# Hybrid attention encoder: scores from 64-row products of two heads in turn, q and k split into high parts and rests without copies

## The chip, the cores and the metric

One core of a Trainium2 chip runs the whole layer in one launch. The metric is the device time of that launch in microseconds (us). TensorE (PE) multiplies, and its weight loads are shown as PEld; VectorE is DVE, ScalarE ACT, GpSimd POOL; SyncE (SP) issues the DMAs.

## What is computed

One encoder layer on two inputs, a sample of 2048 tokens and a prompt of 512, model width 1024, in float32. Cut to what matters here:

```python
h = rms_norm(x, norm_gain)
proj = jnp.einsum('bld,de->ble', h, w_in)        # 9216 columns
# branch a: 2-D neighbourhood attention, 8 heads of 64, window 8 rows x 16 columns, with a bias
q_a, k_a = rms_norm(q), rms_norm(k)
s = einsum(q_a, k_a) / 8 + bias; p = softmax(s); o_a = p @ v
# branch b: three groups (window, dilation) = (128,1), (512,4), (2048,16), 8 heads of 64 each
q, k = rope(rms_norm(q)), rope(rms_norm(k))
s = einsum(q, k) / 8; p = softmax(s) in the band; o = p @ v   # the groups are merged by their lse
br_a = (o_a * silu(g_a)) @ w_branch_a; br_b = (o_b * silu(g_b)) @ w_branch_b
y = x + (sigmoid(m_a) * br_a + sigmoid(m_b) * br_b) @ w_out
```

The norm gains of q and k are large, so scores are computed from split numbers: each of q and k is kept as a high part in fp16 and a rest in fp16, and a score is the sum of three products: high by rest, high by high, rest by high.

## The kernel before

The program is written by a planner: functions are queued by due time in `Clock` (lines 108 to 171), which keeps an estimated time of each engine, and buffers are granted by `Slots` (lines 174 to 236). The calls to matmul, activation and so on are emitted in the order in which the planner runs them, and each engine executes its instructions in that order. PE's estimate for a matmul is columns/2400 + 0.003 us (`mm`, line 350); a change of tile shape is not in it. All matmuls have line 351, most DVE work 364, ACT 359, POOL 376, and the transposing DMAs, which SP issues, line 399 (`turn`).

The stages follow each other on PE. `dil_sweeps` (line 1249): 60 tiles of 128 tokens, each projected to q, k and v (3 banks of 512 columns, 24 matmuls each); `dil_qk` (1358) squares, normalises and ropes q and k, splits them into `qs`, and turns them by DMA into `dq` (queries) and the ring `kT` (keys). `dil_block` (1501) then attends: 30 blocks have 256 keys per query, 36 have 128 (12 of these with only 64 queries). Eight heads make a block, in units of two heads by 256 keys or four heads by 128, so that a unit fills one PSUM bank of 512 columns (`s`, two banks). `na_sweeps` (895): 40 tiles, four heads at a time; `na_qk` (980) and `na_group` (1083), with units of one head by 512 or 384 keys (sample) or two heads by 256 (prompt); the q there is turned into `qn` and reordered by DVE into `qT`. After that `gate_sweeps` (1567) and `out_sweep` (1996) compute no scores.

A unit goes through `head` (764): score matmuls into a bank; DVE adds the mask and takes the maximum (`top`, which frees the bank); ACT takes the exponential; the result is split in two fp16 parts `p`, turned by DMA to `pT`, and multiplied with v into `o` (`pump`, 824). Up to two units are at work between score and reduction, one bank each. A unit's heads have the same parity (0 and 2, say).

The layout of the operands decides the shape of a score matmul. `parts_q` (742) writes q's high part twice for each head, side by side, and the rests of all heads after that; `parts_k` (749) writes for each pair of heads high, rest, rest, high. After the turn, one head of q is 128 partitions (high, high), one head of k 128 partitions (high and rest, in an order that depends on parity). `score` (755) then needs two matmuls: one over 128 rows for high by high plus high by rest, one over the 64 rows of the head's half for rest by high.

Buffers that the change touches (lines 57 to 78): `vc` (gathered v of the neighbourhood sweeps), `dq`, `qs` and `qn`.

Of the kernel before, what the change touches and what calls it, by code (L numbers as in the profile page):

```python
# [13 lines left out]
F32 = mybir.dt.float32  # L14
F32R = mybir.dt.float32r
BF16 = mybir.dt.bfloat16
FP16 = mybir.dt.float16
# [51 lines left out]
NE = 2  # L69
NHB = 2  # L70
NQS = 2
NOSB = 2
NV2 = 1
NQN = 2
NBM = 4
WT = 13
WA = 6
WD = 12
M_T = 0.5
M_L = 1.0  # L80
M_S = 0.0
M_CS = 6.0
NA_STEP = 2.3
NA_LAST = 1.2
NA_P = 0.7
# [22 lines left out]
class Clock:  # L108
# [34 lines left out]
    def first(self, **costs):  # L143

        return min(costs, key=lambda e: max(self.now, self.free[e]) + costs[e])
# [114 lines left out]
def size(ap):  # L260
    return math.prod(ap.shape[1:])


class Enc:


    def __init__(self, ctx, tc, a):
        self.ctx, self.tc, self.nc, self.a = ctx, tc, tc.nc, a
        clk = self.clk = Clock()
# [21 lines left out]
        self.values = deque()  # L291
        self.unit_at = 0.0

    def load_const(self, ap, shape, name):
# [444 lines left out]

    def parts_q(self, x, out, nh):

        x = x.rearrange("p (h d) -> p h d", d=64)
        hi = out[:, 0:128 * nh].rearrange("p (h r d) -> p h r d", r=2, d=64)
        lo = out[:, 128 * nh:192 * nh].rearrange("p (h d) -> p h d", d=64)
        return (hi, x.unsqueeze(2).to_broadcast([128, nh, 2, 64])), (lo, x, hi[:, :, 0])

    def parts_k(self, x, out, nh):

        x = x.rearrange("p (a e d) -> p a e d", e=2, d=64)
        z = out[:, 0:128 * nh].rearrange("p (a z d) -> p a z d", z=4, d=64)
        return (z[:, :, 0::3], x), (z[:, :, 1:3], x, z[:, :, 0::3])

    def score(self, out, q, k, h, sel, m):

        nh = sel
        pp = slice(64 * (h % 2), 64 * (h % 2) + 64)
        self.mm(out, q[:, h, :m], k, True, False)
        self.mm(out, q[pp, nh + h // 2, :m], k[pp], False, True)  # L760

    def head(self, time, u):
# [5 lines left out]
        def score():  # L770
            u["s"] = self.new("s", [128, 512])
            u["scores"](u["s"])
            self.values.append(u)
            clk.then(S["e"].take, top)

        def top():
            e = u["e"] = self.new("e", [128, 512])
# [41 lines left out]
            u["ready"] = True  # L819
            self.pump()  # L820

        clk.at(time, S["s"].take, score)

    def pump(self):

# [154 lines left out]
    def na_qk(self, R, seq, i, ps):  # L980

        clk, S = self.clk, self.S
# [20 lines left out]
            clk.then(S["qs"].take, split)  # L1003

        def split():
            qs = R["qs"] = self.new("qs", [128, 1536], FP16)
            R["q"] = self.parts_q(R["x"][:, 0:256], qs[:, 0:768], 4)
            R["k"] = self.parts_k(R["x"][:, 256:512], qs[:, 768:1280], 4)
            self.gains.when(gain)
            self.act(*R["q"][0])  # L1010
            clk.then(low_q)
# [23 lines left out]
        def turn_q():  # L1035
            if i // 4 not in seq["qT"]:
                seq["qT"][i // 4] = None
                S["qT"].take(new_q)
            R["qn"] = self.new("qn", [128, 6, 128], FP16)
            self.turn(R["qn"], R["qs"][:, 0:768])  # L1040
            moved.signal()
            clk.then(seq["q_gate"][i // 4].when, order)

        def new_q():
            seq["qT"][i // 4] = self.new("qT", [128, 6, 4, 8, 16], FP16, self.N["qT"])
            seq["q_gate"][i // 4].signal()

        def order():
# [7 lines left out]
        def turn_k():  # L1056
            if "kT" not in seq:
                pool, sfx = (self.N["kTs"], "") if tok == 0 else (self.N["kTp"], "p")
                seq["kT"] = pool.tile([128, 4, 64 * seq["rows"]], FP16, name=f"kT{sfx}")
            self.turn(seq["kT"][:, :, 128 * i:128 * i + 128], R["qs"][:, 768:1280])  # L1060
            moved.signal()
            there.signal()

# [19 lines left out]
    def na_group(self, seq, g):  # L1083

        clk, S = self.clk, self.S
        half, tok, rows = seq["half"], seq["tok"], seq["rows"]
        last = rows // 8 - 1
        lo = 0 if g == 0 else 8 * g - 4
        hi = 8 * g + 8 if g == last else 8 * g + 12
        nr = hi - lo  # L1090
# [43 lines left out]
        def unit(time, c, hs):  # L1134
            st = sts[c]
            kc = (0, 8, 24, 32)[c]
            n = 32 * nr
            u = {"m": 128, "n": n, "hs": hs, "first": hs[0] == 0, "v": lambda: st["v"], "sc": self.sc[0], "st": st}
            bm = [bms[(0, 1, 1, 2)[c], h] for h in hs]

            def scores(s):
                q = qT.rearrange("p j c r e -> p j c (r e)")[:, :, c]
                for j, h in enumerate(hs):
                    self.score(s[:, n * j:n * j + n], q, kT[:, h, lo:hi, kc:kc + 32], h, 4, 128)
                    left["scores"] -= 1
                    if left["scores"] == 0:
                        S["qT"].give(qT)
                    seq["scored"].signal()

            def topped():  # L1150
# [40 lines left out]
                if c == 3 and seq["last"]:  # L1191
                    self.na_done.signal()

            u.update(scores=scores, topped=topped, den=den, mask=lambda j: bm[j]["bm"], out=out)
            if hs[-1] == 3:
                u["last"] = lambda: S["osb"].take(finish)

            def go(j=0):
                if j < len(hs):
                    bm[j]["gate"].when(go, j + 1)  # L1200
                else:
                    self.head(0.0, u)

            clk.at(time, go)
# [8 lines left out]
        for c, hs in order:  # L1213
            ct = (0, 1, 1, 2)[c]
            if hs[0] == 0:
                clk.at(t - 5.0, seq["stored"][hi // 2 - 1].when, start, c)
            if c != 2:
                for h in hs:
                    bms[ct, h] = {"uses": 2 if c == 1 else 1, "gate": Gate(clk)}
                    clk.at(t - 3.5, self.bias_ready[half].when, S["bm"].take, bias, ct, h)  # L1220
            unit(t, c, hs)
            t += (NA_LAST if seq["last"] else NA_STEP) * len(hs) * (NA_P if nr == 8 else 1.0)
        self.unit_at = t


# [132 lines left out]
    def dil_qk(self, R, i, ps):  # L1358

        clk, S, H = self.clk, self.S, R["H"]  # L1360
        B = {}
# [40 lines left out]
            clk.then(S["qs"].take, high)  # L1402

        def high():
            B["qs"] = self.new("qs", [128, 1536], FP16)
            B["parts"] = (self.parts_k if i else self.parts_q)(B["x"], B["qs"], 8)
            self.act(*B["parts"][0])
            clk.then(low)

# [4 lines left out]

        def turn():
            for out, rows in R["to", i]():
                self.turn(out, B["qs"][rows, 0:1024 if i else 1536])
            S["qs"].give(B["qs"])
            R["ch"]["done"][R["i"]].signal()

# [9 lines left out]
    def dil_plan(self, R):  # L1430
# [6 lines left out]
            R["place", j] = Gate(clk)  # L1437

        def q_tile():
            return self.new("dq", [128, 12, 128], FP16, self.D["qT"])  # L1440

        def new_k():
            ch["slot"][i] = self.blocks % 4
# [57 lines left out]
    def dil_block(self, R, srcs, m, q, ks, vs, mask, free):  # L1501
# [6 lines left out]
        def unit(h0):  # L1508
# [1 line left out]
            hs = tuple(range(h0, h0 + 2 * nh, 2))  # L1510

            def scores(s):
                for j, h in enumerate(hs):
                    self.score(s[:m, n * j:n * j + n], q(), self.ring[:, h, ks()], h, 8, m)

            def osb():
                if "osb" not in st:
# [8 lines left out]
            def store():  # L1526
# [8 lines left out]
                if self.blocks_left == 0:  # L1535
                    self.dil_done.signal()

            u = {"m": m, "n": n, "hs": hs, "first": h0 == 0, "st": st, "v": vs, "scores": scores, "sc": self.sc[1],
                 "mask": lambda j: mask, "topped": lambda: None, "out": lambda j: st["o"][:, 64 * hs[j]:64 * hs[j] + 64],
                 "mx": lambda: osb()[:m, 512 + h0:511 + h0 + 2 * nh:2], "den": lambda j: osb()[:m, 520 + hs[j]:521 + hs[j]]}  # L1540
            if hs[-1] == 7:
# [94 lines left out]
    def gate_o(self, H, br, blk):  # L1636
# [20 lines left out]
            self.mw_gate.when(self.merge, 2 * blk + tt, o, lambda: clk.then(S["qs"].take, high, tt, o))  # L1657

        def high(tt, o):
            qs = self.new("qs", [128, 1536], FP16)  # L1660
            self.act(qs[:, 0:512], o)
            clk.then(low, tt, o, qs)

# [479 lines left out]
```

## Time and profile before

| | |
|---|---|
| median of 3 runs | 2948.18 us (2947.4 to 2948.27) |
| the profiled execution | 2953.89 us, of which the span from first to last instruction is 2952.1 us |
| mean granted TensorE clock | 0.978 of full speed |
| PE busy | 2799.5 us (20153 matmuls, each with its load) |
| DVE, ACT, POOL busy | 1611.3, 1345.0, 1273.4 us |
| DMA | 429.60 MB, its one large queue at 64.5% of 16 engines' span |

Times count from the first instruction. A row of a group gives the line, the engine, the operation, out<-in by the program's names, the tile of the array for matmuls (128*128 is rows by columns), the shape of what is streamed (128x256: partitions by columns), the count, busy us, mean ns of one, and then the idle time of the engine just before, with what ended it. A matmul's end is modelled, so that what a matmul costs is read from one start to the next. "s" is the bank of scores (and, in the gate sweeps, of another product), "proj" that of projections, "o" that of the attention's output, "mx" the maximum of a reduced score.

### The profile page before, as it was taken

Reading aid. Unit: us, or ns where it says so; the run is one execution under the profiler, and the core shown is the slowest. Engines: PE = TensorE matmul, PEld = TensorE weight load, DVE = VectorE, ACT = ScalarE, POOL = GpSimd, SP = SyncE. Lnnn points to the kernel's source line nnn. Section 1 sums busy time; section 2 is a strip of 40 time slices with the busy share of each in tenths; the row PEclk is TensorE's granted clock in tenths of the full one; section 3 lists DMA queues with packets and bytes.
Section 4 is the critical chain, followed back from the end, with each engine's and each line's share of the span. In section 5 each row is a group of like instructions: output and inputs, shape, how many; then the busy total and the mean of one; then the engine's idle time right before and its main releaser. Section 6 shows DMA issues by size and latency. Waiting matters only on the chain.

```text
span 2952.1 us, 54403 instructions
## 1 busy us (share of the span) xinstructions
PE 2799.5 (95%) x20153; PEld 1821.3 (62%) x20153; DVE 1611.3 (55%) x3894; ACT 1345.0 (46%) x3492; POOL 1273.4 (43%) x1797
## 2 busy tenths in 40 slices
PE   6999999999999999988988788899999999999999
PEld 2444444444444444444545445699999999999887
DVE  6777767776554744336777578622244544444111
ACT  5667666566565655544565466421122211222110
POOL 4777776776767777733555455200001000011110
PEclk9999999999999999999999898899999999999999
DMA  7999996867665765559999999622234443453443
GB/s 230 203 207 195 195 196 116 167 130 126 112 123 109 148 110 104 104 127 187 195 198 196 172 209 200 154 51 65 72 114 119 137 131 109 126 168 107 151 150 107
DMA packets 864459, 429.60 MB, mean 146 GB/s; under 512 B 747200, under 2 KB 791872, under 8 KB 857792
## 3 DMA queue, kind: packets, MB, share of 16 engines
q1 hardware_dynamic: 864192, 426.12, 64.5%
q8 instruction: 158, 2.59, 0.4%
q14 instruction: 109, 0.89, 0.1%
HBM read 171.72 MB, written 79.13 MB: 85 GB/s over the span
## 4 chain that ended last, share of the span: by engine, by line
PE 59%; DVE 6%; DMA 6%; ACT 3%; issue 2%; POOL 1%; SPq 1%; DVEq 0%; ACTq 0%; POOLq 0%
PE proj L351 46%; PE s L351 12%; DMA pT<-p 3%; DVE p L364 2%; PE o L351 2%; DVE e L364 2%; ACT e L359 1%; DMA qn<-qs 1%; DMA hb<-htd 1%; DMA wr<-in_w_in 1%; DMA kT<-qs 1%; SPq L394 1%; DVE wt L364 1%; POOL qk L376 0%; DVE wm L364 0%
## 5 line engine op out<-in xcount | busy, mean ns | idle before, releaser
L351 PEld LDWEIGHTS <-hb 128*128 128x128 f16 x6240 | 577.0, 99 | 601.4 <-issue 50.6
L351 PE MATMUL proj<-wt,hb 128*128 128x512 f16 (+2 forms) x3360 | 702.2, 358 | 14.6 <-DMA hb<-htd 14.6
L351 PE MATMUL proj<-wu,hb 128*128 128x512 f16 x2880 | 670.0, 383 | 11.6 <-DVE wu L364 10.1
L359 ACT ACTIVATE e<-e,neg,sc 128x256 f32<-128x256 f32 (+4 forms) x688 | 394.7, 575 | 11.1 <-DVE neg L364 3.6
L359 ACT ACTIVATE sg<-proj,wi 128x256 f32<-128x256 f32 x240 | 113.2, 473 | 612.5 <-PE proj L351 606.4
L351 PE MATMUL proj<-hb,wt 128*128 128x256 f16 x2760 | 313.8, 273 | 1.6 <-DMA hb<-htd 1.6
L351 PEld LDWEIGHTS <-pT 128*128 128x128 f16 (+1 forms) x4560 | 223.3, 100 | 130.6 <-DMA pT<-p 59.0
L351 PEld LDWEIGHTS <-wt 128*128 128x128 f16 x2760 | 269.0, 98 | 34.7 <-issue 2.6
L364 DVE TENSOR_TENSOR p<-e,p 128x512 f16<-128x512 f32 (+2 forms) x304 | 256.4, 844 | 44.0 <-ACT p L359 41.0
L376 POOL TENSOR_TENSOR sq<-qk,gcs 128x256 f32<-128x256 f32 x240 | 184.0, 788 | 223.3 <-DVE q_ssq L364 212.1
L364 DVE TENSOR_TENSOR qk<-s,sg 128x256 f32<-128x256 f32 x160 | 67.8, 424 | 336.4 <-PE s L351 333.4
L364 DVE CAST p<-e 128x512 f16<-128x512 f32 (+2 forms) x234 | 141.1, 603 | 195.0 <-ACT e L359 170.0
L351 PE MATMUL s<-hb,wt 128*128 128x256 f32 x1880 | 247.1, 285 | 0.0
L351 PE MATMUL proj<-hb,kT 128*128 128x256 f16 x1920 | 228.5, 275 | 5.5 <-DVE kT L364 3.5
L351 PEld LDWEIGHTS s<-hb,wt 128*128 128x128 f32 x1880 | 231.3, 189 | 1.0
L351 PE MATMUL s<-kT,dq 64*128 64x256 f16 (+5 forms) x1056 | 209.3, 254 | 3.0 <-DMA kT<-qs 3.0
L364 DVE CUSTOM_DVE_ANT_0 e<-s,cmask 128x256 f32<-128x256 f32 (+2 forms) x528 | 157.3, 343 | 96.0 <-PE s L351 92.3
L351 PEld LDWEIGHTS <-kT 128*128 128x128 f16 x1920 | 183.9, 99 | 31.6 <-DVE kT L364 5.0
L351 PEld LDWEIGHTS <-dq 64*128 64x128 f16 (+3 forms) x1056 | 101.8, 96 | 136.9 <-issue 54.6
L376 POOL TENSOR_TENSOR hb<-sg,hb 128x256 fp32r<-128x256 f32 x19 | 18.8, 989 | 381.2 <-ACT hb L359 381.1
L376 POOL TENSOR_TENSOR qk<-qk,sq 128x512 f32<-128x512 f32 (+1 forms) x122 | 167.2, 1370 | 34.6 <-DVE qk L364 25.1
L359 ACT ACTIVATE qs<-qk 128x1024 f16<-128x1024 f32 (+1 forms) x200 | 140.3, 706 | 84.0 <-POOL qk L376 65.4
(182 smaller groups left out, 3899.0 us busy)
## 6 DMA issues: line engine op xcount, KB each, us to landing
hb<-htd SPq DMA_DIRECT2D x40, 1024.0 KB
wr<-in_w_in SPq DMA_DIRECT2D x132, 256.0 KB
obd<-osb SPq DMA_DIRECT2D x50, 264.0 KB
hd<-xs SPq DMA_DIRECT2D x20, 512.0 KB
htd<-hb SPq DMA_DIRECT2D x10, 1024.0 KB
mad<-qk SPq DMA_DIRECT2D x40, 256.0 KB
e<-obd SPq DMA_DIRECT2D x40, 256.0 KB
sq<-mad SPq DMA_DIRECT2D x40, 256.0 KB
```

Of the source, the lines that this page charges most:

```text
L351: self.nc.tensor.matmul(out, a, b, start=start, stop=stop)
L359: self.nc.scalar.activation(out, x, func, **kw)
L364: getattr(self.nc.vector, ins)(out, *a, **kw)
L376: getattr(self.nc.gpsimd, ins)(out, *a, **kw)
L394: self.nc.sync.dma_start(out=out, in_=in_)
```

## The change

q and k are each split once into high parts of all heads and rests of all heads, without the second copies (`parts` takes the place of `parts_q` and `parts_k`; 1024 columns for 8 heads in both, where q had 1536). Each score is three matmuls over 64 rows, high by rest, high by high, rest by high. `head` now takes two units, of even and odd heads, whose matmuls alternate between the lower and the upper 64 rows and between the two banks; both banks are taken before the first matmul. The neighbourhood units are paired likewise (heads 0 and 1, 2 and 3; in the prompt (0, 2) with (1, 3)). The planner counts half of a matmul's time for one of a pair, and 0.3 us for each pair. Four buffers are deeper. Functions that only follow the new shapes (`qs`, `qn`, `qT`, `dq` with 1024, 4, 4 and 8 in place of 1536, 6, 6 and 12) are left out here.

```diff
-NVC = 3
+NVC = 4
-NDQ = 4
+NDQ = 6
-NQS = 2
+NQS = 3
-NQN = 2
+NQN = 3
+SWITCH = 0.3
...
-    def mm(self, out, a, b, start, stop):
-        self.nc.tensor.matmul(out, a, b, start=start, stop=stop)
-        self.clk.pe(size(b) * (4 if b.dtype == F32 else 1) / 2400 + 0.003)
+    def mm(self, out, a, b, start, stop, share=1, **kw):
+        self.nc.tensor.matmul(out, a, b, start=start, stop=stop, **kw)
+        self.clk.pe((size(b) * (4 if b.dtype == F32 else 1) / 2400 + 0.003) / share)
...
+    def parts(self, x, out, nh):
+        hi, lo = out[:, 0:64 * nh], out[:, 64 * nh:128 * nh]
+        return (hi, x), (lo, x, hi)
+
+    def score(self, banks):
+        for j in range(max(len(b) for b in banks)):
+            for i, (x, y) in enumerate(((0, 1), (0, 0), (1, 0))):
+                for bank in banks:
+                    out, q, k, h, n, m = bank[j]
+                    pp, c = slice(64 * (h % 2), 64 * (h % 2) + 64), h // 2
+                    self.mm(out, q[pp, c + x * (n // 2), :m], k[pp, c + y * (n // 2)], i == 0 and j == 0, i == 2,
+                            share=len(banks), skip_group_check=True)
+        self.clk.pe(SWITCH)
...
+    def head(self, time, *us):
+        clk, S = self.clk, self.S
+        def score():
+            self.score([u["scores"](u["s"]) for u in us])
+            for u in us:
+                u["scored"]()
+                self.values.append(u)
+                clk.then(S["e"].take, self.softmax, u)
+        def first():
+            us[0]["s"] = self.new("s", [128, 512])
+            if len(us) == 1:
+                score()
+            else:
+                S["s"].take(second)
+        def second():
+            us[1]["s"] = self.new("s", [128, 512])
+            score()
+            self.pairs.popleft()
+            if self.pairs:
+                clk.then(S["s"].take, self.pairs[0])
...
         if nr == 8:
-            order = [(c, (e, 2 + e)) for c, e in ((0, 0), (0, 1), (1, 0), (2, 0), (1, 1), (2, 1), (3, 0), (3, 1))]
+            order = [(c, ((0, 2), (1, 3))) for c in range(4)]
         else:
-            order = [(c, (h,)) for c, h in
-                     ((0, 0), (0, 1), (0, 2), (0, 3), (1, 0), (1, 1), (2, 0), (2, 1), (1, 2), (1, 3), (2, 2), (2, 3),
-                      (3, 0), (3, 1), (3, 2), (3, 3))]
+            order = [(c, ((h,), (h + 1,))) for c, h in ((0, 0), (0, 2), (1, 0), (2, 0), (1, 2), (2, 2), (3, 0), (3, 2))]
...
-        clk.at(t, S["osb"].take, lambda: [self.head(clk.now + step * j, u) for j, u in enumerate(us)])
+        clk.at(t, S["osb"].take, lambda: [self.head(clk.now + step * j, *us[j:j + 2]) for j in range(0, len(us), 2)])
```

What followed `score` in `head` before is now `softmax`, one unit at a time and otherwise the same.

## Rows read from the trace of the kernel before

**Rows 1.** Page, span and part 1: busy time, share of the span, instructions.
```profile
span 2952.1 us, 54403 instructions
PE 2799.5 (95%) x20153; PEld 1821.3 (62%) x20153; DVE 1611.3 (55%) x3894; ACT 1345.0 (46%) x3492; POOL 1273.4 (43%) x1797
```

**Rows 2.** Busy time by stretch, all engines.
```profile
core 0: us, PE busy (x) PEld busy (x) DVE busy (x) ACT busy (x) POOL busy (x), PEclk, DMA share, GB/s
170.00:450.00 280.00, 273.21 (x1823) 128.80 (x1821) 201.69 (x469) 194.85 (x507) 201.30 (x276) 1.00 0.92 191
450.00:1260.00 810.00, 801.77 (x5047) 384.93 (x5047) 464.83 (x1260) 489.07 (x1383) 590.59 (x855) 0.99 0.65 122
1260.00:1895.00 635.00, 538.20 (x4243) 303.53 (x4242) 442.11 (x1091) 353.05 (x938) 293.68 (x458) 0.92 0.92 185
1895.00:2952.00 1057.00, 1053.37 (x8372) 944.79 (x8369) 377.97 (x798) 199.80 (x423) 81.71 (x70) 1.00 0.38 115
```

**Rows 3.** Chain that ended last, shares by line: 450 to 1260, then 1400 to 1895 us.
```profile
by line: PE proj L351 45.6%; PE s L351 9.7%; ACT e L359 3.8%; PE o L351 3.6%; issue 2.3%; DMA kT<-qs 1.8%; DVE p L364 1.8%; DVE e L364 1.7%; POOL qk L376 1.6%; SPq L399 0.9%; ACT qs L359 0.8%; DVE wt L364 0.7%; DVE q_ssq L364 0.7%; DVE qs L
...
by line: PE proj L351 18.3%; DMA pT<-p 15.4%; issue 8.5%; DVE p L364 7.1%; DVE e L364 6.3%; PE s L351 5.2%; DMA qn<-qs 4.8%; PE o L351 3.3%; DMA hb<-htd 3.0%; SPq L394 2.0%; DVE qT L364 1.9%; DVE oparts L364 1.8%; ACT e L359 1.7%; POOL q_t 
```

**Rows 4.** Timeline of PE, dilated sweep: start us, us, instructions.
```profile
485.43 3.40 PE L351 MATMUL proj<-wt,hb 128*128 128x512 f16 x15
488.67 0.91 PE L351 MATMUL s<-kT,dq 128*128 128x256 f16 x4
489.51 0.82 PE L351 MATMUL proj<-wt,hb 128*128 128x512 f16 x3
490.17 0.86 PE L351 MATMUL o<-dv,pT 128*128 128x64 f16 x24
```

**Rows 5.** Timeline of PE: a unit of 128 columns, then one of 512.
```profile
905.58 1.34 PE L351 MATMUL s<-kT,dq 128*128 128x128 f16 x8
906.85 2.76 PE L351 MATMUL proj<-wu,hb 128*128 128x512 f16 x12
...
1442.54 0.69 PE L351 MATMUL s<-kT,qT 128*128 128x512 f16 x2
1443.16 0.52 PE L351 MATMUL o<-vc,pT 128*128 128x64 f16 x12
```

**Rows 6.** Groups by form, PEld: busy us, mean ns.
```profile
L351 PEld LDWEIGHTS <-pT 128*128 128x128 f16 x4272 | 212.4, 99 | 120.1 <-DMA pT<-p 57.6 <-issue 11.2
```

**Rows 7.** Score matmuls (tile s) on PE by stretch: span, busy (count).
```profile
170.00:450.00 280.00, 50.12 (x227) 1.00 0.92 191
450.00:1260.00 810.00, 138.14 (x726) 0.99 0.65 122
1260.00:1895.00 635.00, 106.72 (x360) 0.92 0.92 185
```

**Rows 8.** PE's waits, 450 to 1260 us: us, times, longest.
```profile
PE proj L351 <- DVE wm L364: 3.0, 1, 3.0
PE s L351 <- DMA kT<-qs: 3.0, 4, 1.7
PE o L351 <- DMA pT<-p: 1.9, 2, 1.1
PE proj L355 <- DVE wm L364: 0.3, 1, 0.3
```

**Rows 9.** Groups by form, ACT.
```profile
L359 ACT ACTIVATE qs<-qk 128x1024 f16<-128x1024 f32 x60 | 62.9, 1048 | 43.2 <-POOL qk L376 38.7 <-DMA cs<-in_cs 4.5
```

**Rows 10.** Issue of turns on SP, 1260 to 1895 us: ns min/median/max.
```profile
L399 SPq DMA_TRANSPOSE qn<-qs x40: 1210/1243/5965, 1304.4 to 1815.5; - x40
L399 SPq DMA_TRANSPOSE kT<-qs x34: 1188/1221/2437, 1263.9 to 1763.0; - x34
```

**Rows 11.** PE's waits, 1400 to 1895 us.
```profile
PE s L351 <- DVE mx L364: 26.9, 32, 2.5
```

**Rows 12.** Groups by form, DVE: the reduction of a score.
```profile
L364 DVE CUSTOM_DVE_ANT_0 e<-s,cmask 128x256 f32<-128x256 f32 x240 | 91.3, 416 | 34.4 <-PE s L351 32.6 <-DVE p L364 0.5
```

More of the change, by code (lines that the diff above doesn't have):

```diff
@@ L290, in __init__ @@
         self.gains, self.normed = Gate(clk), Gate(clk, NTOK // 128)
-        self.values = deque()
+        self.values, self.pairs = deque(), deque()
         self.unit_at = 0.0
@@ L738, in split_v @@
         self.S[name].take(high)
[L742 to L764, printed above, removed]
+    def parts(self, x, out, nh):
[10 more added lines that the diff above has]
+        self.clk.pe(SWITCH)
@@ new lines, in head, with queue @@
+    def head(self, time, *us):
[18 more added lines that the diff above has]
+                clk.then(S["s"].take, self.pairs[0])
+        def queue():
+            self.pairs.append(first)
+            if len(self.pairs) == 1:
+                S["s"].take(first)
+        if len(us) == 1:
+            clk.at(time, S["s"].take, first)
+        else:
+            clk.at(time, queue)
@@ L766, in head, with softmax @@
+    def softmax(self, u):
         clk, S, m, n, nh = self.clk, self.S, u["m"], u["n"], len(u["hs"])
@@ L768, in head @@
         inv, ninv = (u["sc"][:m, i:i + 1] for i in range(2))
[L770 to L774, printed above, removed]
         def top():
@@ L820, in ready @@
             self.pump()
-        clk.at(time, S["s"].take, score)
+        top()
     def pump(self):
@@ L1005, in split @@
         def split():
-            qs = R["qs"] = self.new("qs", [128, 1536], FP16)
-            R["q"] = self.parts_q(R["x"][:, 0:256], qs[:, 0:768], 4)
-            R["k"] = self.parts_k(R["x"][:, 256:512], qs[:, 768:1280], 4)
+            qs = R["qs"] = self.new("qs", [128, 1024], FP16)
+            R["q"] = self.parts(R["x"][:, 0:256], qs[:, 0:512], 4)
+            R["k"] = self.parts(R["x"][:, 256:512], qs[:, 512:1024], 4)
             self.gains.when(gain)
@@ L1038, in turn_q @@
                 S["qT"].take(new_q)
-            R["qn"] = self.new("qn", [128, 6, 128], FP16)
-            self.turn(R["qn"], R["qs"][:, 0:768])
+            R["qn"] = self.new("qn", [128, 4, 128], FP16)
+            self.turn(R["qn"], R["qs"][:, 0:512])
             moved.signal()
@@ L1044, in new_q @@
         def new_q():
-            seq["qT"][i // 4] = self.new("qT", [128, 6, 4, 8, 16], FP16, self.N["qT"])
+            seq["qT"][i // 4] = self.new("qT", [128, 4, 4, 8, 16], FP16, self.N["qT"])
             seq["q_gate"][i // 4].signal()
@@ L1059, in turn_k @@
                 seq["kT"] = pool.tile([128, 4, 64 * seq["rows"]], FP16, name=f"kT{sfx}")
-            self.turn(seq["kT"][:, :, 128 * i:128 * i + 128], R["qs"][:, 768:1280])
+            self.turn(seq["kT"][:, :, 128 * i:128 * i + 128], R["qs"][:, 512:1024])
             moved.signal()
@@ L1132, in bias, with unit @@
             bms[ctype, h]["gate"].signal()
-        def unit(time, c, hs):
+        def unit(c, hs):
             st = sts[c]
@@ L1137, in unit, with scored @@
             n = 32 * nr
-            u = {"m": 128, "n": n, "hs": hs, "first": hs[0] == 0, "v": lambda: st["v"], "sc": self.sc[0], "st": st}
             bm = [bms[(0, 1, 1, 2)[c], h] for h in hs]
+            u = {"m": 128, "n": n, "hs": hs, "first": hs[0] == 0, "v": lambda: st["v"], "sc": self.sc[0], "st": st,
+                 "bm": bm}
             def scores(s):
                 q = qT.rearrange("p j c r e -> p j c (r e)")[:, :, c]
[L1143 to L1147, printed above, removed]
+                return [(s[:, n * j:n * j + n], q, kT[:, :, lo:hi, kc:kc + 32], h, 4, 128) for j, h in enumerate(hs)]
+            def scored():
+                left["scores"] -= len(hs)
+                if left["scores"] == 0:
+                    S["qT"].give(qT)
+                for _ in hs:
                     seq["scored"].signal()
@@ L1192, in store, with go @@
                     self.na_done.signal()
-            u.update(scores=scores, topped=topped, den=den, mask=lambda j: bm[j]["bm"], out=out)
+            u.update(scores=scores, scored=scored, topped=topped, den=den, mask=lambda j: bm[j]["bm"], out=out)
             if hs[-1] == 3:
                 u["last"] = lambda: S["osb"].take(finish)
[L1198 to L1204, printed above, removed]
+            return u
+        def go(us, bs):
+            if bs:
+                bs[0]["gate"].when(go, us, bs[1:])
+            else:
+                self.head(0.0, *us)
         if nr == 8:
-            order = [(c, (e, 2 + e)) for c, e in ((0, 0), (0, 1), (1, 0), (2, 0), (1, 1), (2, 1), (3, 0), (3, 1))]
+            order = [(c, ((0, 2), (1, 3))) for c in range(4)]
         else:
-            order = [(c, (h,)) for c, h in
-                     ((0, 0), (0, 1), (0, 2), (0, 3), (1, 0), (1, 1), (2, 0), (2, 1), (1, 2), (1, 3), (2, 2), (2, 3),
-                      (3, 0), (3, 1), (3, 2), (3, 3))]
+            order = [(c, ((h,), (h + 1,))) for c, h in ((0, 0), (0, 2), (1, 0), (2, 0), (1, 2), (2, 2), (3, 0), (3, 2))]
         t = max(clk.done + 2.0, self.unit_at)
-        for c, hs in order:
+        for c, units in order:
             ct = (0, 1, 1, 2)[c]
-            if hs[0] == 0:
+            if units[0][0] == 0:
                 clk.at(t - 5.0, seq["stored"][hi // 2 - 1].when, start, c)
             if c != 2:
-                for h in hs:
+                for h in sum(units, ()):
                     bms[ct, h] = {"uses": 2 if c == 1 else 1, "gate": Gate(clk)}
                     clk.at(t - 3.5, self.bias_ready[half].when, S["bm"].take, bias, ct, h)
-            unit(t, c, hs)
-            t += (NA_LAST if seq["last"] else NA_STEP) * len(hs) * (NA_P if nr == 8 else 1.0)
+            us = [unit(c, hs) for hs in units]
+            clk.at(t, go, us, [b for u in us for b in u["bm"]])
+            t += (NA_LAST if seq["last"] else NA_STEP) * (4 * NA_P if nr == 8 else 2.0)
         self.unit_at = t
@@ L1404, in high @@
         def high():
-            B["qs"] = self.new("qs", [128, 1536], FP16)
-            B["parts"] = (self.parts_k if i else self.parts_q)(B["x"], B["qs"], 8)
+            B["qs"] = self.new("qs", [128, 1024], FP16)
+            B["parts"] = self.parts(B["x"], B["qs"], 8)
             self.act(*B["parts"][0])
@@ L1416, in turn @@
             for out, rows in R["to", i]():
-                self.turn(out, B["qs"][rows, 0:1024 if i else 1536])
+                self.turn(out, B["qs"][rows])
             S["qs"].give(B["qs"])
@@ L1439, in q_tile @@
         def q_tile():
-            return self.new("dq", [128, 12, 128], FP16, self.D["qT"])
+            return self.new("dq", [128, 8, 128], FP16, self.D["qT"])
         def new_k():
@@ L1512, in scores @@
             def scores(s):
-                for j, h in enumerate(hs):
-                    self.score(s[:m, n * j:n * j + n], q(), self.ring[:, h, ks()], h, 8, m)
+                return [(s[:m, n * j:n * j + n], q(), self.ring[:, :, ks()], h, 8, m) for j, h in enumerate(hs)]
             def osb():
@@ L1538, in unit @@
             u = {"m": m, "n": n, "hs": hs, "first": h0 == 0, "st": st, "v": vs, "scores": scores, "sc": self.sc[1],
+                 "scored": lambda: None,
                  "mask": lambda j: mask, "topped": lambda: None, "out": lambda j: st["o"][:, 64 * hs[j]:64 * hs[j] + 64],
@@ L1659, in high @@
         def high(tt, o):
-            qs = self.new("qs", [128, 1536], FP16)
+            qs = self.new("qs", [128, 1024], FP16)
             self.act(qs[:, 0:512], o)
```

## The prediction

> **What bounds the kernel now.** I read the page first: span 2952.1 us, PE busy 95% of it, the next engine 55% [rows 1]. A mean over stages says little, so next the table by stretch [rows 2]. From 170 to 1260 us run the dilated sweeps: PE is busy 273 of 280 us, then 802 of 810, while POOL, the next engine, has 591 of 810 and DMA 0.65; before 450 us DMA stands at 0.92. From 1260 to 1895 us run the neighbourhood sweeps: PE 538 of 635, DVE 442, DMA 0.92. After 1895 us come the gate and output sweeps, which score nothing: 1057 us that the change leaves alone. The chain that ended last agrees: in 450 to 1260 us its largest parts are the projections at 45.6% and the scores at 9.7%; in 1400 to 1895 us it hops between the turned p (a DMA, 15.4%), DVE and PE [rows 3]. So PE time saved in the dilated sweeps should come off the end; in the neighbourhood sweeps only a part of it can.
>
> Then the timeline of PE, start to start, since a matmul's end is modelled. Fifteen projection matmuls of 512 columns start 485.43 and end their turn at 488.67: 216 ns each, 213 of it streaming at the 2.4 GHz that the granted clock of 1.00 [rows 2] stands for. The next four matmuls, one score unit of two heads by 256 columns, take 0.84 us to the next projection, 210 ns each where streaming needs 107. **Half of a score's time is not streaming** [rows 4]. What differs is the tile of the array: a head is one 128-row matmul and one 64-row matmul, so every score matmul is followed by one of another shape. It is so in every unit: 8 matmuls of 128 columns take 1.27 us (159 ns against 53), two of 512 take 0.62 us (310 against 213) [rows 5]. Each change of shape costs about 0.1 us; with 1056 + 320 score matmuls that is some 145 us.
>
> **The change, part by part.** *Scores.* Before, in units: 120 of 4x256 at 0.84 us, 48 of 8x128 at 1.27, 24 of the same with 64 queries, taken alike: 192 us in the dilated sweeps. Neighbourhood: 64 of 2x512 at 0.62, 64 of 2x384 at 0.52 (two times 160 ns and two changes), 16 of 4x256 at 0.84: 86 us. After, a pair of units holds only 64-row matmuls: it pays a change going in and one coming out, 0.21 us, and three matmuls per head. Whether the two row halves stream at once no row shows; the bounds are both halves together (two heads in three streamings) and one after the other (six). Together, a pair of 256-column units takes 12/2 x 107 ns + 0.21 = 0.85 us against 1.68; of 128-column units 24/2 x 53 ns + 0.21 = 0.85 against 2.54; of 512-column units 6/2 x 213 ns + 0.21 = 0.85 against 1.24; of 384-column units 0.69 against 1.04. With 60 + 36 dilated pairs that is 82 us, **110 saved**; with 32 + 32 + 8 neighbourhood pairs 56 us, 30 saved. One after the other: 1.49 us a pair (384 columns 1.17), dilated 143 us, 49 saved; neighbourhood 97, a loss of 11. I take together: the two matmuls use other rows, other partitions of q and k and other banks, and no row shows anything that they share; both ends stay for the range.
>
> More loads of weights come with it (2064 for 1376). Their nearest row is the pT load, 99 ns each; yet 24 o matmuls, each with its load (loads and matmuls count alike [rows 1]), are over in 0.86 us, at most 36 ns each [rows 4, 6]: loads hide behind matmuls of their own rows, so I cost them at nothing; uncovered, about 0.1 us a step (a rival below). There the trace differs from a rule of the Trainium skill (TensorE: Matmul & The Clock Gate, Part 3, The mechanism), by which a load overlaps a running matmul only where its row group is another; by that rule the third and later loads of a pair would wait, which is that rival's sum. The same section's table has four row tiles at 3.07 times one, not 4; an estimate from it, 1.53 for two, would leave some 19 us of the dilated saving unmade; no run here shows it.
>
> *Where it counts.* Of the 1056 dilated score matmuls, 227 stand in 170 to 450 us and 726 in 450 to 1260; 40 of the 360 of the last stretch are dilated too [rows 7], the other 63 lie before 170 us. By share of the 110: 24, 76, 4 and 6. The 6 fall into the start, before the sweeps run evenly: I count nothing there, 6 at most. Of the 24 I count half, since DMA at 0.92 can follow little faster; of the 76 all, for all that PE waits for there are four kinds, 8.2 us [rows 8]. With half of the 4: **90 us**. Of the neighbourhood 30 I count **10** with the lighter turns below, as PE is only one of three loaded resources there.
>
> *Rests without copies.* The 60 copies of dilated q on ACT write half as much: at 1048 ns each [rows 9] at most 31 us of ACT, which is busy 489 of 810 us [rows 2]; cover, so nothing. Turned q falls from 12 to 8 column blocks (6 to 4 in the neighbourhood sweeps). SP's issue gains nothing: 768 columns took 1243 ns to issue, k's 512 took 1221 [rows 10]. DMA moves 40 x 256 x 128 x 2 bytes = 2.6 MB less in a stretch that moved 185 GB/s x 635 us = 117 MB [rows 2]: 2%, at most 14 us if DMA bounds all of it, nothing if latency does; I take 4 of the 10 above from it.
>
> *Deeper buffers* (vc, dq, qs, qn) let transfers start earlier and issue nothing new. They gain between nothing and the 4.8% of 495 us that the chain spends on turned q, 24 us [rows 3]; I take nothing, since the data comes no sooner.
>
> *The new wait.* A pair's scores need both banks, so both units of the pair before must have been reduced. Behind a waiting score matmul PE's whole queue stands. Before, PE waited for that 32 times, 26.9 us, all in the neighbourhood sweeps [rows 11]. With less slack on PE as well, I put 8 us of new waits, between 0 and, if every pair waited through a neighbour's reduction, the price in the third rival.
>
> Sum: 90 + 10 - 8 = 92 us off. The profiled execution took 2953.9 us, 5.7 above the median of 2948.18, 0.2%; so 2862 by its own time and **2856** against the runs.
>
> **Rivals.** (1) *The halves don't pack.* One after the other: dilated 49 saved, of which 0.82 lands by the shares above (90 of 110), 40; neighbourhood 0 net; 8 new waits: 32, so 2916. Or the loads stand uncovered, 0.1 us for each of 6, 12 or 3 steps a pair: 0.6 x 60 + 1.2 x 36 = 79 of the 110 are gone, 25 of the rest land, some 5 come from the neighbourhood sweeps, 8 are waited: 22, so 2926. For it: no row shows 64-row matmuls in sequence; against the second: the o rows. This is also the case of a change that does only half of what it says. (2) *Another engine takes PE's place in the dilated sweeps.* POOL would be busy 591 of 734 us, 81%, and its rope feeds every q and k; half of the 90 stays: 45 + 10 - 8 = 47, so 2901. For it: the order is fixed by a planner that counts no change of shape, so PE has so far run late against it and others had slack; against: PE's waits are 8 of 810 us there [rows 8]. (3) *Slower: both banks at once.* A pair waits for DVE to reduce the pair before, four heads of 256 at 416 ns and more [rows 12]: 1.7 us. If each of 168 pairs waits that long on PE, 286 us are lost against 100 gained: 3134; if half the pairs do, 143: 2991. It decides from 0.6 us a pair on (100/168). Against it: none of the four waits of 450 to 1260 us is for mx [rows 8]; for it: DVE's 442 of 635 us in the neighbourhood sweeps.
>
> **How the numbers follow.** Forecast 0.56, its own range 2806 to 2893 (below: 20 more of the neighbourhood 30, 10 more of DMA's 14, the other 12 of the 24 and no waits, 50 in all; above: 19 us of pairs that pack worse and 18 of waits). Rival 1 0.18, rival 2 0.16, rival 3 0.10. The range 2800 to 2926 holds the forecast and rivals 1 and 2, so some 0.85 with what each may miss. A measurement here tells 0.2%, 6 us, from no change. Faster: 0.56 + 0.16 + 0.15 of rival 1 = 0.87; same 0.04; slower 0.09 from rival 3 where most of its pairs wait.
>
> **What would show it.** Packed: a 4x256 pair's 12 score matmuls within about 0.85 us, the s busy time of 450 to 1260 us (138 us [rows 7]) about halved, that stretch some 75 us shorter and the gate sweeps the same. Unpacked: the same pair 1.5 us. Uncovered loads: gaps of 0.1 us between steps. Rival 2: new PE waits for kT, dq or proj. Rival 3: PE s waiting for DVE's mx in the dilated sweeps. A neighbourhood stretch that grows, or moves by over 40 us, would make me wrong there.

## The result: 35 us of some 92

The changed kernel took 2913.73 us (median of 4 runs, 2907.35 to 2914.12) beside 2948.22 us before: a ratio of 0.9875, 95% interval 0.9858 to 0.9892. The profiled execution took 2913.82 us. It lies in the range, but 35 us off is well under half of the 92 forecast. One of the four executions of experiment 2 took 9170.77 us; it is in the median given there and not in the ratio. The page after, span, part 1 and the chain by engine, then the chain of before:

```profile
span 2912.0 us, 55755 instructions
PE 2687.4 (92%) x20841; PEld 1785.7 (61%) x20841; DVE 1627.4 (56%) x3902; ACT 1303.5 (45%) x3495; POOL 1269.4 (44%) x1787
PE 46%; DVE 15%; POOL 14%; ACT 9%; DMA 8%; issue 6%; SPq 2%; DVEq 0%; ACTq 0%; POOLq 0%
```

```profile
PE 59%; DVE 6%; DMA 6%; ACT 3%; issue 2%; POOL 1%; SPq 1%; DVEq 0%; ACTq 0%; POOLq 0%
```

PE's share of the chain is 46%, and DVE, POOL and ACT have 15, 14 and 9; before, they had 59, 6, 1 and 3, in a chain that was followed through 78% of the span only. Next, the score matmuls (durations ns min/median/max, then first and last start), before and after:

```profile
L351 PE MATMUL s<-kT,dq x1056: 216/243/421, 79.3 to 1304.1; 128*128 128x256 f16 x80, 128*128 128x128 f16 x64, 128*64 128x128 f16 x32
L351 PE MATMUL s<-kTp,qT x64: 269/280/421, 1565.4 to 1877.2; 128*128 128x256 f16 x32, 64*128 64x256 f16 x32
```

```profile
L352 PE MATMUL s<-kT,dq x1584: 213/227/418, 77.1 to 1265.7; 64*128 64x256 f16 x90, 64*128 64x128 f16 x72, 64*64 64x128 f16 x36
L352 PE MATMUL s<-kTp,qT x96: 266/269/390, 1530.1 to 1837.3; 64*128 64x256 f16 x96
```

The last dilated score starts at 1304 us before and at 1266 after: 38 us earlier. From there to the last neighbourhood score it is 573 us before and 572 after, and the gate and output sweeps are the same work. So **the dilated sweeps hold all of the gain**, and the neighbourhood sweeps gave nothing.

**The packing does what it says.** PE's timeline after, in the stretch of [rows 4]:

```profile
487.40 0.83 PE L352 MATMUL s<-kT,dq 64*128 64x256 f16 x12
488.16 2.12 PE L352 MATMUL proj<-wt,hb 128*128 128x512 f16 x9
...
493.64 0.82 PE L352 MATMUL o<-dv,pT 128*128 128x64 f16 x12 [2.07 <-DMA pT<-p]
494.27 1.47 PE L352 MATMUL proj<-wv,hb 128*128 128x512 f16 x3
495.68 1.46 PE L352 MATMUL s<-kT,dq 64*128 64x256 f16 x12
497.07 0.52 PE L352 MATMUL o<-dv,pT 128*128 128x64 f16 x12
...
503.05 0.86 PE L352 MATMUL s<-kT,dq 64*64 64x128 f16 x24
503.84 0.52 PE L352 MATMUL o<-dv,pT 128*128 128x64 f16 x12
```

Twelve matmuls of 256 columns, four heads, take 0.76 us to the next start (487.40 to 488.16); with the change of shape in front of them, some 0.1 us that fall on the projection before, that is the 0.85 forecast, for 1.68 before. Of 54 such pairs the median is 0.76 us. Twelve streamings one after another would need 1.28 us, so the two halves do stream together. 24 of 128 columns take 0.79 (503.05). Loads are hidden too: a row half gets a new one before each of its matmuls, and there are no gaps. Then the stretch from 170 us to the last dilated score, all engines (columns as in [rows 2]), first before, then after:

```profile
170.00:1304.00 1134.00, 1109.06 (x7075) 530.97 (x7073) 683.87 (x1778) 703.99 (x1952) 808.54 (x1159) 0.99 0.71 139
```

```profile
170.00:1266.00 1096.00, 1014.43 (x7509) 494.69 (x7508) 683.61 (x1748) 674.69 (x1949) 805.40 (x1158) 0.98 0.68 137
```

PE is busy 1109 us before and 1014 after, 95 us less, near what the forecast freed here (24 + 76 + 4 = 104 by its shares). But it stood idle 25 us (1134 - 1109) and now 82 (1096 - 1014): **57 us came back as waits**, and 95 - 57 = 38 is the whole result. PE's waits in these two stretches (us in total, times, longest), before, then after:

```profile
PE o L351 <- DMA pT<-p: 10.8, 12, 2.9
PE proj L351 <- DMA hb<-htd: 7.0, 1, 7.0
...
```

```profile
PE o L352 <- DMA pT<-p: 48.3, 36, 4.3
PE proj L356 <- DVE wm L365: 12.2, 5, 4.7
PE s L352 <- DVE osb L365: 9.9, 17, 2.4
PE s L352 <- DMA kT<-qs: 9.0, 8, 3.0
...
```

Most are for turned p: 10.8 us have become 48.3. Upstream, ACT's and DVE's queues show what moved. ACT and DVE before, then both after:

```profile
ACT neg L359 <- DVE osb L364: 215.4, 133, 4.8
ACT qk L359 <- PE proj L351: 51.8, 30, 4.7
ACT qs L359 <- POOL qk L376: 47.2, 26, 5.3
...
```

```profile
DVE qs L364 <- ACT qs L359: 38.9, 26, 5.2
```

```profile
ACT qs L360 <- POOL qk L377: 160.5, 67, 6.7
ACT neg L360 <- DVE osb L365: 139.0, 130, 6.8
...
ACT qk L360 <- PE proj L352: 26.1, 18, 3.1
...
```

```profile
DVE qs L365 <- ACT qs L360: 110.0, 51, 7.4
```

ACT's split of q and k (qs) waits for the rope on POOL 160 us where it was 47, and the exponentials stand behind it in ACT's queue; DVE's rests wait for ACT in turn, 110 us for 39. ACT's waits for PE's projections halve, and those for DVE's maxima (neg) fall from 215 to 139. POOL is no busier (809 and 805 us), and ACT is idle as long as before (1134 - 704 = 430 us, then 1096 - 675 = 421); what has changed is who arrives last. So this table doesn't show that the wait for the rope makes PE's 57 us, and run 10 below speaks against it in part.

### The profile page after: what moved, and what is told of

Same layout as the page of the kernel before. It is cut to its first block, busy times and chain, and to the rows that moved or that the text cites. A ratio compares the mean times of both kernels' runs of the same rounds, so it can differ in the third digit from the quotient of the medians.

```text
span 2912.0 us, 55755 instructions
## 1 busy us (share of the span) xinstructions
PE 2687.4 (92%) x20841; PEld 1785.7 (61%) x20841; DVE 1627.4 (56%) x3902; ACT 1303.5 (45%) x3495; POOL 1269.4 (44%) x1787
## 4 chain that ended last, share of the span: by engine, by line
PE 46%; DVE 15%; POOL 14%; ACT 9%; DMA 8%; issue 6%; SPq 2%; DVEq 0%; ACTq 0%; POOLq 0%
PE proj L352 36%; PE s L352 9%; POOL qk L377 7%; ACT e L360 5%; DVE e L365 4%; DMA pT<-p 4%; DVE p L365 3%; POOL sq L377 3%; POOL q_t L377 2%; DVE wm L365 1%; DVE q_ssq L365 1%; DMA qn<-qs 1%; ACT qs L360 1%; DVE qs L365 1%; DMA wr<-in_w_in 1%
## 5 line engine op out<-in xcount | busy, mean ns | idle before, releaser
L352 PEld LDWEIGHTS <-hb 128*128 128x128 f16 x6240 | 590.7, 99 | 615.9 <-issue 68.7
L352 PE MATMUL proj<-wt,hb 128*128 128x512 f16 (+2 forms) x3360 | 694.0, 359 | 5.8 <-DVE v L365 4.5
L365 DVE TENSOR_TENSOR p<-e,p 128x512 f16<-128x512 f32 (+2 forms) x302 | 265.6, 883 | 27.1 <-ACT p L360 22.3
L365 DVE CAST p<-e 128x512 f16<-128x512 f32 (+2 forms) x237 | 151.2, 639 | 168.8 <-ACT e L360 151.5
L360 ACT ACTIVATE qs<-qk 128x512 f16<-128x512 f32 (+1 forms) x200 | 106.8, 537 | 208.3 <-POOL qk L377 188.5
L365 DVE TENSOR_TENSOR qs<-qk,qs 128x512 f16<-128x512 f32 (+1 forms) x169 | 122.8, 730 | 135.6 <-ACT qs L360 133.8
L377 POOL TENSOR_TENSOR qk<-qk,gcs 128x512 f32<-128x512 f32 x120 | 162.0, 1350 | 9.4
```

Source lines behind the costliest of these rows:

```text
L352: self.nc.tensor.matmul(out, a, b, start=start, stop=stop, **kw)
L360: self.nc.scalar.activation(out, x, func, **kw)
L365: getattr(self.nc.vector, ins)(out, *a, **kw)
L377: getattr(self.nc.gpsimd, ins)(out, *a, **kw)
```

## Experiments

Two theories came first. P: POOL's rope is late and ACT and DVE queue behind it. L: the planner just sets the o matmuls too early on PE. Beside them B (a pair's two banks cost the time) and D (deeper buffers made the gain). Times are medians of 4 runs or more; ratios are to before on the same chip, with 95% intervals, and a difference from the changed kernel is that of the two ratios times 2948.

**1. The rope's last step left out.**

```diff
-            self.pool("tensor_tensor", x, x, sq, op=ALU.add)
```

> Leaves out the rope's last step, the add of the two products, so q and k of the dilated sweeps are the cosine product alone: 120 POOL instructions of 1.37 us, 165 us of POOL, are gone; everything else of the changed kernel stays. Theory P (packing freed some 112 us of PE in the dilated sweeps, and 59 of them came back as waits because POOL's rope is late and ACT's and DVE's queues stand behind it): the waits shrink, 2855 to 2885 us. Rival L (the planner only sets the o matmuls too early) and rival B (a pair's two banks cost the time): POOL is off the path, 2905 to 2918 us.

2882.24 us, 0.9761 (0.9742 to 0.978), 34 us under the changed kernel, as P had it, and against L and B. POOL's step counts, then, although POOL is busy only 73% of the stretch (805 of 1096 us). But the planner no longer counts the step either: from 100 us on PE's turns stand in another order, and the 34 us hold both, the work and the order.

**2. The o matmuls later.**

```diff
-M_PV = 1.5
+M_PV = 4.0
```

> The planner's margin between the turned p and the o matmuls on PE goes from 1.5 to 4.0 us, nothing else. Rival L: most of the 44 us that PE waits for the turned p in the dilated sweeps is gone, 2875 to 2895 us. Theory P: the same lateness meets PE at another matmul, or the o banks and turned buffers run short; the o waits fall but the time stays within 10 us of 2914.

2935.88 us, 0.9942 (0.9925 to 0.9958): 20 us slower than the changed kernel. PE's waits from 170 us to its last dilated score:

```profile
PE s L352 <- DVE osb L365: 31.9, 34, 5.6
PE proj L356 <- DVE wm L365: 17.6, 6, 5.6
PE s L352 <- DMA kT<-qs: 14.9, 9, 4.8
PE o L352 <- DMA pT<-p: 12.3, 15, 2.6
...
```

The wait for p fell from 48 us to 12, and others rose in its place: the scores' for the reduction of the pair before (DVE osb: in these sweeps the maxima lie in `osb`) from 10 to 32, the weights' wm from 12 to 18, kT from 9 to 15. L falls as it was put; the move of the waits was expected by P, the 20 us by neither.

**3. One unit and one bank at a time.** The three products of a head come one after the other, on one row half and in one bank.

```diff
-                self.head(0.0, *us)
+                for u in us:
+                    self.head(0.0, u)
...
-        clk.at(t, S["osb"].take, lambda: [self.head(clk.now + step * j, *us[j:j + 2]) for j in range(0, len(us), 2)])
+        clk.at(t, S["osb"].take, lambda: [self.head(clk.now + step * j, u) for j, u in enumerate(us)])
```

> Units go one at a time into one bank, as before the change, with the three 64-row products of each head one after the other: nothing overlaps. By rows, PE needs 163 us for the dilated scores where pairs need 82, and 112 for the neighbourhood scores where pairs need 56. Theory P: PE has idle time in the dilated sweeps that takes a part of that, so 20 to 60 us slower than the changed kernel, 2935 to 2975 us. Rival B (waiting for two banks costs what packing gains): at most 10 us slower, or faster, up to 2924 us.

2979.65 us, 1.0096 (1.0081 to 1.0111): 65 us slower than the pairs, a little more than P expected, and 28 slower than before. That is against B, and so are PE's own waits for a pair's banks in the changed kernel, 9.9 us (DVE osb above). A unit on PE's timeline, then two that stand back to back in the neighbourhood sweeps:

```profile
808.15 0.82 PE L352 MATMUL s<-kT,dq 64*128 64x256 f16 x6
808.90 1.47 PE L352 MATMUL proj<-wv,hb 128*128 128x512 f16 x6
...
1463.88 0.83 PE L352 MATMUL s<-kT,qT 64*128 64x512 f16 x6
1464.64 0.82 PE L352 MATMUL proj<-wt,hb 128*128 128x512 f16 x3
```

Six matmuls of 256 columns take 0.75 us here; in a pair twelve do in 0.76: **two row halves are worth exactly two**. In the neighbourhood sweeps units of an even and an odd head can follow each other directly, and there they overlap in run 3 too: six matmuls of 512 columns take 0.76 us (1463.88), where one after the other would need 1.28. So what makes them stream together is not that the program alternates them. The rest of run 3's cost is to be sought in the dilated sweeps, where units stand apart. There is a hint in it: with 0.75 + 0.1 us a unit PE has no more to do for these scores than before (0.84), for 128 columns less, and still the kernel is slower than before. Its plan counts 0.96 us for such a unit (6 x 256 columns and `SWITCH`), where the old one counted 0.44; so a part of the 65 us can be the order's, which the next runs take up.

**4. The old depths.**

```diff
-NVC = 4
+NVC = 3
...
-NDQ = 6
+NDQ = 4
...
-NQS = 3
+NQS = 2
...
-NQN = 3
+NQN = 2
```

> The four buffers back to their old depths (vc 3, dq 4, qs 2, qn 2), scores packed as in the changed kernel. Theory P: depth is not what moved the time, 2910 to 2925 us. Rival D (the gain of 34 us comes from deeper buffers): 2935 us or more.

2919.32 us, 0.9896 (0.9879 to 0.9912): deeper buffers are worth some 6 us, which the two intervals don't tell from nothing. D is out.

**5 to 8. Is it the order?** The planner writes the order from estimated times. Theory S: the old plan left out the changes of shape, so PE ran later than planned and the other engines had slack; C: the hand-overs bind whatever the plan.

```diff
# 5, the changed kernel
-        self.clk.pe((size(b) * (4 if b.dtype == F32 else 1) / 2400 + 0.003) / share)
+        self.clk.pe((size(b) * (4 if b.dtype == F32 else 1) / 2200 + 0.003) / share)
# 6, the kernel before
         self.mm(out, q[:, h, :m], k, True, False)
+        self.clk.pe(0.1)
         self.mm(out, q[pp, nh + h // 2, :m], k[pp], False, True)
+        self.clk.pe(0.1)
# 7, the changed kernel
-        self.clk.run("P", 0.15 + (n or size(out)) / 480)
+        self.clk.run("P", 0.2 + (n or size(out)) / 440)
# 8, the changed kernel
-            self.pool("tensor_tensor", x3, x3, B["y"].unsqueeze(2).to_broadcast([128, 8, 64]), op=ALU.mult)
+            self.vec("tensor_tensor", x3, x3, B["y"].unsqueeze(2).to_broadcast([128, 8, 64]), op=ALU.mult)
```

> The planner's estimate of a matmul goes from columns/2400 to columns/2200 us, so that it sets other engines' work against a PE that is 9% slower than it is, about as late as the changes of tile shape made it before the change. What is computed is the same, only the order differs. Theory S (the old order had slack because PE ran late against the plan, and the packed scores took it away): the new waits shrink, 2880 to 2902 us. Theory C (POOL, ACT and DVE bound the dilated sweeps by what they hand each other, whatever the plan): 2904 to 2924 us.

> The kernel before the change, with 0.1 us more in the planner's PE estimate after each score matmul: the plan now counts the changes of shape that the old plan left out. Theory S: the old order loses its slack and the kernel gets 10 to 40 us slower than before, 2958 to 2990 us. Theory C: the same as before within 8 us.

> The planner's POOL estimate goes from 0.15 + n/480 to 0.2 + n/440 us, which is what the trace shows (1.36 us for 512 elements where the plan says 1.22). Theory S: ACT and DVE are no longer queued behind a rope that is not ready, 2885 to 2905 us. Theory C: 2905 to 2924 us.

> The rope's scaling of q and k by the inverse norm goes from POOL to DVE: 120 instructions of 1.15 us less on POOL, as many of some 0.75 us more on DVE. Theory C: the hand-overs get shorter, as in the run without the add, 2885 to 2905 us. If DVE is the tighter of the two, 2915 us or more; theory S alone says within 10 us of 2914.

Run 5: 2974.49 us, 1.0077 (1.0061 to 1.0093), 60 us slower than the changed kernel with the same instructions in another order. Run 6: 2992.17 us, 1.0137 (1.0119 to 1.0155): **the old kernel loses 40 us when its plan is told the truth about PE.** Run 7: 2901.12 us, 0.9827 (0.9811 to 0.9844), 14 us off, as S expected. Run 8: 2959.23 us, 1.0033 (1.0022 to 1.0044), 47 us slower: DVE cannot take POOL's work in this order.

Runs 5 and 6 both raise the plan's PE times, and both are slower, so S had the right cause and, for run 5, the wrong sign: a plan that thinks PE slow puts fewer of PE's other matmuls ahead of a score or o matmul, and PE gets there early. Where the plan counts PE too low, as the old one did, it puts more in front, and the rest has time. Run 6 from 170 us to its last dilated score:

```profile
170.00:1334.00 1164.00, 1109.05 (x6998) 527.64 (x6996) 661.96 (x1759) 700.10 (x1950) 800.52 (x1159) 0.99 0.68 135
```

PE's busy time is that of before (1109 us); it stands idle 55 us (1164 - 1109) for 25, and these 30 us are waits.

**9 to 12. Slack given back (S2).** Four heads of 256 columns needed 1.68 us of PE before, where eight matmuls at 256/2400 + 0.003 us made 0.88 in the plan; in the changed kernel they need 0.85, where twelve halves and `SWITCH` make 0.96. Run 11 is run 10 with run 7's POOL estimate; run 12 is that estimate in the kernel before.

```diff
# 9, the changed kernel
-        self.clk.pe((size(b) * (4 if b.dtype == F32 else 1) / 2400 + 0.003) / share)
+        self.clk.pe((size(b) * (4 if b.dtype == F32 else 1) / 2640 + 0.003) / share)
# 10 and 11, the changed kernel
-SWITCH = 0.3
+SWITCH = -0.6
# 11, and 12 in the kernel before
-        self.clk.run("P", 0.15 + (n or size(out)) / 480)
+        self.clk.run("P", 0.2 + (n or size(out)) / 440)
```

> The opposite sign of the run with columns/2200: the changed kernel with columns/2640 in the planner, so that it places each score and o matmul behind 10% more of PE's other work and PE meets them later against the other engines. Theory S2 (what counts is how much later PE is in truth than in the plan; the old plan left out the changes of shape, half of a score's time, and so gave each chain of softmax that slack; the new plan counts a pair in full): 2870 to 2900 us. Theory C (the hand-overs of POOL, ACT and DVE bound the dilated sweeps whatever the order): 2905 to 2925 us.

> Only the planner's cost of a pair changes, SWITCH from 0.3 to -0.6 us: a pair of 4x256 counts 0.06 us against 0.85 in truth, a shortfall of 0.8 us for four heads, about what the old plan left out (0.88 planned, 1.68 in truth). Theory S2: the old slack is back with the packed scores, 2865 to 2895 us. Theory C: 2905 to 2925 us.

> The run before, with the planner's POOL estimate at 0.2 + n/440 us as well. If the two mend different waits, another 8 to 15 us come off against SWITCH -0.6 alone; if both only add slack to the same chains, it is within 6 us of it.

> The kernel before the change with the planner's POOL estimate at 0.2 + n/440 us. If POOL's lateness against the plan came up only with the packed scores (theory S2: PE was late enough to hide it), the old kernel does not gain: within 6 us of before. If POOL's estimate was a fault of its own, it gains 8 to 15 us here too.

Run 9: 2880.99 us, 0.9765 (0.9751 to 0.978). Run 10: **2871.84 us, 0.9736 (0.9722 to 0.9751)**, 41 us under the changed kernel and 78 under before, by one constant of the planner. Run 11: 2879.67 us, 0.976 (0.9743 to 0.9776), 7 us above run 10, intervals overlapping, just outside both its expectations: no more to get from POOL's estimate. Run 12: 2946.86 us, 0.999 (0.9981 to 1.0): next to none to get before the change. S2 held in advance in runs 9, 10 and 12, and C, by which the order would not matter, falls. A count in the traces agrees with S2: in the mean of the 192 units of the dilated sweeps, PE runs 52 projection matmuls between a unit's scores and its own o matmuls before, and 49 in run 6; 55 in the changed kernel, 51 in run 5, 60 and 59 in runs 9 and 10 (the n-th unit is set against the n-th twelve o matmuls). The slower order of each kernel has fewer, these two faster ones more; run 7, 14 us faster, has 55 as well, so the count is not all of it. What is not shown is that the shortfall has to lie on the scores: runs 7 and 9 gain by other constants, and a planner whose constants had been fitted to the old kernel would look much the same. Run 10, its scores, the dilated stretch and PE's waits in it:

```profile
L352 PE MATMUL s<-kT,dq x1584: 212/216/280, 79.2 to 1220.7; 64*128 64x256 f16 x90, 64*128 64x128 f16 x72, 64*64 64x128 f16 x36
L352 PE MATMUL s<-kTp,qT x96: 266/269/418, 1511.7 to 1795.9; 64*128 64x256 f16 x96
```

```profile
170.00:1221.00 1051.00, 999.19 (x7517) 490.26 (x7515) 697.64 (x1757) 665.33 (x1930) 821.82 (x1155) 0.99 0.72 143
```

```profile
PE o L352 <- DMA pT<-p: 24.0, 33, 2.8
PE proj L356 <- DVE wm L365: 8.4, 5, 4.0
...
```

```profile
ACT qs L360 <- POOL qk L377: 136.2, 67, 7.0
```

The last dilated score starts at 1221 us, 83 before the old one, and PE stands idle 52 us (1051 - 999) instead of 82; it is also busy 15 us less for the same matmuls (the last section). From there to the last neighbourhood score (1796) it is 575 us, as ever. The last line is ACT's wait for the rope: still 136 us, while PE has 30 us of its waits back. So that wait does not set PE's loss by itself.

**13 and 14. The rest.** Run 13 has the edits of 9 and 10, run 14 those of 10 and 1 (the rope's add left out).

```diff
-SWITCH = 0.3
+SWITCH = -0.6
# 13
-        self.clk.pe((size(b) * (4 if b.dtype == F32 else 1) / 2400 + 0.003) / share)
+        self.clk.pe((size(b) * (4 if b.dtype == F32 else 1) / 2640 + 0.003) / share)
# 14
-            self.pool("tensor_tensor", x, x, sq, op=ALU.add)
```

> SWITCH -0.6 and columns/2640 together: more slack than either. If the lost slack is all mended by SWITCH -0.6, nothing is left to gain, 2866 to 2885 us; if the waits that remain in the dilated sweeps (some 50 us) are lack of slack too, 2840 to 2864 us.

> SWITCH -0.6 and the rope's last add left out (q and k of the dilated sweeps are the cosine product alone; 165 us of POOL gone). If PE bounds the dilated sweeps again once the order leaves slack, POOL's work hardly counts: within 10 us of 2872. If POOL's hand-overs still hold the sweeps back, as they did under the changed kernel's order (31 us came off there), 20 us or more come off here too, 2852 us or less.

Run 13: 2903.62 us, 0.9846 (0.9828 to 0.9865), 32 us slower than run 10: neither expectation held. Too much slack costs as well (62 projection matmuls by the count above); in the dilated sweeps PE now waits for ACT to read the projections' banks:

```profile
PE proj L352 <- ACT sq L360: 40.9, 14, 4.7
...
```

Run 14: 2835.46 us, 0.9619 (0.9595 to 0.9643), 34 us under run 10, as the second expectation had it. Without the rope's last step 34 us go under either estimate of a pair, so its work is most likely a cost of its own, beside the slack. It is not shown apart: like run 1, run 14 also takes the step out of the plan, and its order is not run 10's. Run 14 from 170 us to its last dilated score, and what is left of ACT's wait for the rope:

```profile
170.00:1180.00 1010.00, 983.62 (x7426) 485.50 (x7425) 640.64 (x1738) 652.87 (x1900) 656.88 (x1038) 0.99 0.73 147
```

```profile
ACT qs L360 <- POOL qk L377: 71.0, 31, 5.1
```

PE stands idle 26 us there (1010 - 984), as before the change.

## Why the prediction was wrong

- *The bound, the 0.1 us per change of shape, the 0.85 us a pair*: right (0.76 and the change in front). That both halves stream together and loads are covered, the choice with no row behind it, was right: rival 1 is out. The Trainium skill's rule by which a load waits for a matmul of its own row group (TensorE: Matmul & The Clock Gate, Part 3, The mechanism) does not agree with the 12 matmuls in 0.76 us, nor with the six on one row half in 0.75 of run 3. An estimate from a table of the same page of the Trainium skill (Part 3, Measured speedup vs the span model), 1.53 for two row tiles, does not agree with the 2.0 measured here.
- *"Of the 76 all", and 8 us of new waits*: **this is the step that failed.** All that PE waits for before were 8 us in 450 to 1260 us, and I read that as room in the other engines. It was room that the order had put there, because its planner counted half of what a score took PE. The change speeds PE up and mends the estimate in one go, and both use up the same slack: 57 us of new waits where the forecast had 8. Run 10 splits them: with the estimate lowered, PE is idle 52 us for 82, so 30 of the 57 are the order's. The other 27 are gone only where the rope's last step is left out as well (run 14, idle 26 us); whether it is POOL's work that does it or the order that changes with it stays open. Rival 2 named this, with POOL's rope as the place and the planner as the reason, but at 0.16 and a loss of half, 2901; it was 2914. POOL's load, which it gave as 81%, was 73% and no more work than before; ACT's wait behind POOL grew from 47 to 160 us, but 136 of it are left in run 10.
- *Neighbourhood 10 us*: it came to 1 or 2, and to none in run 10: 573, 572 and 575 us in three orders say that the scores on PE are not what sets that stretch. Over all fourteen experiments it lies between 568 and 583. What does set it was not tried. PE's waits there, a second line of the view of [rows 11], then 1360 to 1855 us after:

```profile
PE o L351 <- DMA pT<-p: 29.2, 19, 7.7
```

```profile
PE s L352 <- DVE mx L365: 39.0, 46, 3.1
PE o L352 <- DMA pT<-p: 33.8, 24, 5.7
...
```

- *Buffers at nothing*: some 6 us, not clear of noise. *Rests without copies*: not tried alone.
- *Rival 3*: a pair's wait for both banks is there, 9.9 us in 17 waits in the dilated sweeps (DVE osb; 7.5 in run 3, where units go singly) and 39.0 for 26.9 in the neighbourhood sweeps, but far from 0.6 us a pair, and run 3 is slower.
- With slack given back (run 10) the change gives 78 of the 92 us; of the missing 14, 10 are what was counted for the neighbourhood sweeps.

## What to carry to other kernels

A change of tile shape on TensorE between small matmuls can cost as much as the matmuls; keep one shape for a burst, and let two 64-row products in two banks stream together. Where the order is planned from estimates, small waits on the busiest engine show slack only as long as that order stands: before counting freed time as gained, look at which queues hand work to each other in order, and when a step gets faster, tune the planner's cost for it by runs: the true cost was not the best one here.

## What was not expected of the hardware

A wait of 2.1 us seems to cost more than itself. In the timeline above PE waits until 493.64; the three projection matmuls at 494.27 are through at 495.68, 1.41 us with the change of shape in it, where three at 216 ns and 0.1 make 0.75, and the same pair of 12 then takes 1.39 us for 0.76. The granted clock around it (8 us in the middle):

```profile
480.00:490.00 10.00, 10.00 (x77) 4.95 (x76) 7.32 (x17) 7.00 (x19) 7.10 (x10) 1.00 0.59 111
490.00:498.00 8.00, 5.93 (x50) 2.79 (x48) 4.93 (x16) 5.15 (x16) 6.79 (x10) 0.79 0.99 191
498.00:508.00 10.00, 10.00 (x99) 5.30 (x97) 7.16 (x25) 6.96 (x23) 8.27 (x12) 1.00 0.66 106
```

0.79 over the middle stretch, the level of 1.2 GHz for a part of it, after PE had stood still. Over the dilated sweeps the clock is 0.98 for 0.99, and the same matmuls keep PE busy 1014 us in the changed kernel and 999 in run 10, where the clock is 0.99 and the waits are fewer. That fits a lower clock after waits; it was not tried by itself.
